# Where the tiles lie: pool order and two fillers in a hybrid attention layer

## The chip, the cores and the metric

The kernel runs on one core of a Trainium2 chip. A time is the device time of one execution in microseconds (us), and the figure compared is the median over runs. TensorE is the matrix engine: a matmul streams its moving operand, up to 512 columns, through a stationary operand ("the weights") that a separate instruction has loaded before. The weights of the next matmul are loaded while the present one streams.

## The reference

One decoder layer over 2048 tokens with 1024 channels, with 16 learned meta tokens ahead of them, all in float32:

```python
xn = rms_norm(h, norm_gain[l])
proj = xn @ w_in[l]
sb_q, sb_k, sb_v, sw_q, sw_k, sw_v, sb_z, sw_z, g_sb, g_sw = jnp.split(proj, offsets, axis=-1)
o_sb = stick_breaking_attention(sb_q, sb_k, sb_v, valid)       # 8 heads of 64, all earlier keys
q, k = rope(sw_q, pos), rope(sw_k, pos)
o_sw = sliding_window_sink_attention(q, k, sw_v, sinks, valid) # 16 query heads, 2 key heads, 128 keys
y_sb = (o_sb * jax.nn.silu(sb_z)) @ w_branch_sb[l]
y_sw = (o_sw * jax.nn.silu(sw_z)) @ w_branch_swa[l]
merged = jax.nn.sigmoid(g_sb) * y_sb + jax.nn.sigmoid(g_sw) * y_sw
h = h + merged @ w_out[l]
return rms_norm(h, final_norm_gain)
```

(The heads' reshapes are left out.) The stick-breaking attention weighs each key by sigmoid(z) times the product of one minus sigmoid(z) over all nearer keys.

## The kernel before, in words

**Precision.** Every large operand is split into a high and a low part (`xh` and `xl`, `wh` and `wl`, and so on), and a product takes three matmuls: low and high of the moving operand with `wh`, and high with `wl` (L400 to L402 in `gemm`). A product of 1024 channels is 8 blocks of three, 24 matmuls of 512 columns.

**Stages.** Tokens come in four groups of 512, in two halves of two groups.
- The opening normalizes the first groups and makes the first keys, queries and values. For a part of it the moving operands are `uh` and `ul`, the rows not yet scaled, in the pool `start`.
- Each half then has a window stage (pool `swa0` or `swa1`): the projections run as the main stream, and `weave` inserts the sliding-window attention between their blocks. Its matmuls are the scores (L695, moving `kk`, weights `q`), transposes of the scores `sc` (L724, moving `ident`) and the values (L741, moving `ph`, `pl`, `ch`, `cl`, weights `vv` for two and difference tiles `xs` for the other two).
- Then a stick stage (pool `sb0` or `sb1`): the gates' projections are the main stream, and the stick-breaking attention is woven in. Its matmuls are the scores (L838, moving `kt`, weights `q1` and `q2`), transposes of `row` (L860), and the values (L886, moving `wth` and `wtl`, weights `vc`).
- The finish, for both halves, projects the two branches (L222 to L224, moving `ringl` for the window branch and `ringr` for the other, weights `wh` and `wl`), merges them into `ringl`, and multiplies by the output weights (L279 to L281, weights `ringl`, moving `ringr`).

**Order.** TensorE's order is written out by hand over the whole program; so is VectorE's until early in the first window stage, and ScalarE's and SP's in the opening. The rest is ordered by a scheduler. SP issues all of the data transfers from one queue.

**Where tiles lie.** A pool hands out places in the order in which its tiles are first asked for, and pools are stacked: `const`, then one of `start`, `swa0`, `sb0`, `swa1`, `sb1` and the finish's `cl` on the left side; `w`, `x`, `tmp` and the finish's `wb` on the right. So what stands at the end of `const` shifts all of the left pools. The right side's `xh`, `xl`, `wh` and `wl` lie at 480 modulo 512 bytes, and `ringr` at 160. `const` ends at 320, and from there the sizes of the tiles set the rest; `row` and `sc` are not whole multiples of 512 bytes long, so each of their buffers lies elsewhere.

Of the kernel before, what the change touches and what calls it, by code (L numbers as in the profile page):

```python
# [7 lines left out]
F32 = mybir.dt.float32  # L8
F32R = mybir.dt.float32r
# [7 lines left out]
P = 128  # L17
# [3 lines left out]
NM = 16  # L21
GT = 512
# [5 lines left out]
QB = 4  # L28
# [11 lines left out]
def f32(ap):  # L40
    return ap.bitcast(F32)
# [3 lines left out]
def tile_kernel(ctx, tc, x, xt, meta, metat, gain, w_in, w_sb, w_sw, w_out, sinks, fgain,  # L45
# [8 lines left out]
    def DMA(dst, src):  # L54
        nc.sync.dma_start(*(t.bitcast(F32) if t.dtype == F32R else t for t in (dst, src)))

    ctx.enter_context(tc.manual_schedule(engines={mybir.EngineType.PE}))
    cp = ctx.enter_context(tc.tile_pool(name="const", bufs=1, side="left"))
# [19 lines left out]
    vn = cp.tile([P, 4], F32, name="vn")  # L78
    vf = cp.tile([P, 16], F32, name="vf")
    mx = cp.tile([P, KT, 48], F32R, name="mx")  # L80
    for t in (vm, mx):
        V.memset(f32(t), 0.0)

# [509 lines left out]
    def window(half, groups, sp):  # L593
# [3 lines left out]
        sn = sp.tile([P, 2 * GT], F32, name="sn")  # L597
        DMA(ct, cost[:, groups[0] * GT:(groups[0] + 2) * GT])
        DMA(sn, sint[:, groups[0] * GT:(groups[0] + 2) * GT])
        if half == 0:  # L600
            cm = sp.tile([P, NM], F32, name="cm")
            sm = sp.tile([P, NM], F32, name="sm")
            DMA(cm, cost[:, SEQ:])
            DMA(sm, sint[:, SEQ:])
            G.memset(f32(kk[:, :, 8 * P:]), 0.0)
            G.memset(f32(vv[:, 8]), 0.0)
        else:
            DMA(kk[:, :, 8 * P:], ksv)
            DMA(vv[:, 8].rearrange("p a d -> p (a d)"), vsv)
# [167 lines left out]
    def stick(groups, bp, sums_of={}):  # L777
        kt, vc = {}, {}
        rows_of = {}
        for g in groups:  # L780
            w = wm[g % 2]
            G.memset(f32(w), 1.0)
            G.affine_select(out=w, in_=f32(w), pattern=[[-1, 4], [0, P]], compare_op=ALU.is_equal, fill=0.0,
                            base=-64 - 4 * g, channel_multiplier=1)
        av_todo = []

        def load_kv(h, g):

            p, a = divmod(h, 2)
            r = slice(64 * a, 64 * a + 64)  # L790
            if h not in kt:
                kt[h] = bp.tile([P, (4 - groups[0]) * GT + NM], F32R, tag="k", name="kt", bufs=2)
            for c in range(g, 4):
                if (h, c) in vc:
                    continue
                c0 = (c - groups[0]) * GT
                cs = slice(c0, c0 + GT + (NM if c == 3 else 0))
                DMA(kt[h][0:64, cs], kd[p][c][0][r])
                DMA(kt[h][64:128, cs], kd[p][c][1][r])
                v = vc[h, c] = bp.tile([P, 4, P], F32R, tag="v", name="vc", bufs=5)  # L800
                DMA(v, vd[p][c][a])
# [13 lines left out]
        def row(h, g, n, j):  # L815

            if n == j == 0:
                load_kv(h, g)
                state[h, g] = {"q": load_q(h, g), "last": {}}
                n1 = len(state) - 1  # L820
                for g1, ssq in list(sums_of.items())[n1 // 8:n1 // 8 + 1]:
                    i, f = divmod(n1 % 8, 2)
                    t = bp.tile([P, GT], F32, tag="q2", name="xq", bufs=2)
                    DMA(t, x[g1 * GT + i * P:g1 * GT + (i + 1) * P, f * GT:(f + 1) * GT])
                    A.activation(t, t, AF.Square, accum_out=ssq[:, f, i:i + 1])
# [70 lines left out]
        n = len(steps)  # L896
        turned = []
        for s in range(n + LT + 3):
# [3 lines left out]
            t = s - LT  # L902
# [181 lines left out]
    for half, groups in enumerate(halves):  # L1084
        with tc.tile_pool(name=f"swa{half}", bufs=1, side="left") as sp:
# [8 lines left out]
            if m:  # L1094
                late_consts()
            sw_k, sw_v, sw_q, attend, ending = window(half, groups, sp)
            q = [[lambda p=p: sw_q(p) for p in (2 * s, 2 * s + 1)] for s in range(4)]
            steps = [(s, g) for s in range(4) for g in groups]
# [26 lines left out]
        with tc.tile_pool(name=f"sb{half}", bufs=1, side="left") as bp:  # L1125
            vsplit[0] = False
            next_sums = {g: sums() for g in halves[1]} if half == 0 else {}
            side = stick(groups, bp, next_sums)
            drain(tiles_by_tile(gts[3:4], groups))
            rest = 25 if half == 0 else 23  # L1130
            cost_sb = 8 * sum(4 * (4 - g) for g in groups) * 1.31 + 16 * 0.75
            ratio = cost_sb / ((rest - 4) * 10.4)
            weave(tiles_by_tile(gts[4:rest], groups), side, ratio)
            drain(side)
            if half == 0:
                t, u = (bp.tile([P, GT], F32, tag="wh", name="sum", bufs=3)[:, :8] for _ in range(2))
                for n, ssq in enumerate(next_sums.values()):
                    V.tensor_tensor(t[:, 4 * n:4 * n + 4], ssq[:, 0], ssq[:, 1], op=ALU.add)
                rs = tp.tile([P, 8], F32, tag="rs8", name="rs", bufs=1)
                rsqrt(rs, t, tp, t=u)  # L1140
                rs0, rs1 = rs[:, :4], rs[:, 4:]
# [72 lines left out]
```

## Time and profile before

| what | value |
|---|---|
| median of 3 runs | 2178.58 us (2178.47 to 2178.74) |
| profiled execution: span, first to last instruction | 2176.8 us |
| what the runs' median has beside the span | 1.8 us |
| TensorE busy | 2148.2 us, 99% |
| VectorE, ScalarE, GpSimd busy | 1355.8, 1007.0, 372.1 us |
| granted TensorE clock, mean | 0.999 |
| opening and first window stage | to about 365 us |
| first gates alone and first stick stage | 365 to 765 us |
| gates and projections, then second window stage | 765 to 1121 us |
| second stick stage | to 1657 us |
| last gates alone | 1657 to 1720 us |
| finish | 1720 us to the end |

A group of instructions is given as line, engine, operation, tiles, shapes and count; then busy time, the mean duration of one in ns, and the idle time ahead of them with what ended it. A row of the timeline gives the start in us, the duration, and the same names. The duration of a matmul includes a modelled end that overlaps the next one, so the time that a matmul costs is the step from its start to the next one's start, not its duration; of two groups of the same shape, though, durations show which one steps faster.

### The profile page before, as it was taken

What the parts mean: (1) busy time and instruction counts of PE and PEld (TensorE: products, weight loads), DVE (VectorE), ACT (ScalarE), POOL (GpSimd) and SP (SyncE); (2) the same over time, 40 slices, a digit from 0 to 9 for tenths busy, and PEclk for the clock granted to TensorE, in tenths of its full rate; (3) what the DMA queues carried; (4) which work ended last, traced back from release to release, by engine and by line L of the source; (5) the groups of instructions that cost most, each with busy time, mean ns of one, the idle gap of its engine ahead of it and who ended that gap; (6) DMA issues with size and microseconds to landing.
All of it is one profiled execution on the core that took longest, in us unless ns stands there. A gap on an engine that the chain in (4) does not pass through costs nothing.

```text
span 2176.8 us, 30232 instructions
## 1 busy us (share of the span) xinstructions
PE 2148.2 (99%) x10614; PEld 1766.2 (81%) x10614; DVE 1355.8 (62%) x2117; ACT 1007.0 (46%) x2328; POOL 372.1 (17%) x486
## 2 busy tenths in 40 slices
PE   8999999999999999999999999999999999999998
PEld 6778888888888888888877888888888888887886
DVE  7687875456555443777746888878774436553453
ACT  6577774344434434777744555555553202221121
POOL 2233342332223200222310000000000232000000
PEclk9999999999999999999999999999999999999999
DMA  9755455765555465444365443333323986468532
GB/s 334 262 179 189 171 188 183 253 200 200 182 187 182 153 203 158 142 165 148 124 193 163 119 122 112 119 100 104 117 85 126 356 276 195 167 218 277 155 97 87
DMA packets 174648, 380.41 MB, mean 175 GB/s; under 512 B 22912, under 2 KB 41088, under 8 KB 174496
## 3 DMA queue, kind: packets, MB, share of 16 engines
q1 hardware_dynamic: 174496, 378.48, 52.2%
q8 instruction: 84, 1.38, 0.3%
q14 instruction: 68, 0.56, 0.1%
HBM read 237.35 MB, written 140.98 MB: 174 GB/s over the span
## 4 chain that ended last, share of the span: by engine, by line
PE 90%; DMA 3%; ACT 3%; DVE 3%; issue 1%; POOL 0%; SPq 0%; ACTq 0%; DVEq 0%; POOLq 0%
PE ps_g L400 15%; PE ps_g L401 14%; PE ps_g L402 14%; PE ps_o L886 6%; PE ps_z L838 6%; PE ps_t L860 5%; PE ps_o L741 2%; PE ps_z L695 2%; PE ps_g L223 1%; PE ps_g L224 1%; PE ps_z L224 1%; PE ps_z L223 1%; PE ps_z L222 1%; PE ps_g L222 1%; PE ps_t L224 1%
## 5 line engine op out<-in xcount | busy, mean ns | idle before, releaser
L400 PE MATMUL ps_g<-xh,wh 128*128 128x512 f32 x1544 | 638.0, 413 | 8.0 <-ACT xh L936 7.6
L402 PE MATMUL ps_g<-xh,wl 128*128 128x512 f32 x1544 | 608.1, 394 | 0.6 <-DVE wl L108 0.6
L401 PE MATMUL ps_g<-xl,wh 128*128 128x512 f32 x1544 | 608.1, 394 | 0.0
L849 DVE TENSOR_TENSOR_SCAN row<-row 128x512 f32<-128x512 f32 (+2 forms) x320 | 371.2, 1162 | 168.8 <-POOL row L847 98.3
L402 PEld LDWEIGHTS ps_g<-xh,wl 128*128 128x128 f32 x1544 | 290.8, 188 | 66.1 <-DVE wl L108 1.1
L400 PEld LDWEIGHTS ps_g<-xh,wh 128*128 128x128 f32 x1544 | 292.2, 189 | 55.2 <-ACT xh L936 7.6
L401 PEld LDWEIGHTS ps_g<-xl,wh 128*128 128x128 f32 x1544 | 292.3, 189 | 43.8 <-DVE xl L937 1.3
L842 ACT ACTIVATE row<-ps_z 128x512 f32<-128x512 f32 (+1 forms) x320 | 171.9, 538 | 251.3 <-PE ps_z L838 208.4
L112 DVE SCALAR_TENSOR_TENSOR wtl<-ps_t,wth 128x512 fp32r<-128x512 f32 (+1 forms) x320 | 190.0, 594 | 46.5 <-ACT wth L111 45.1
L111 ACT ACTIVATE wth<-ps_t 128x512 fp32r<-128x512 f32 (+1 forms) x320 | 170.2, 532 | 91.4 <-PE ps_t L860 89.8
L838 PE MATMUL ps_z<-kt,q 128*128 128x512 f32 (+3 forms) x640 | 185.2, 370 | 0.3 <-ACT row L842 0.3
L860 PE MATMUL ps_t<-ident,row 128*128 128x128 f32 x1088 | 171.7, 273 | 1.2 <-DVE row L849 1.2
L860 PEld LDWEIGHTS ps_t<-ident,row 128*128 128x128 f32 x1088 | 135.9, 140 | 37.3 <-DVE row L849 1.7
L847 POOL TENSOR_SCALAR_AFFINE_SELECT row<-row 128x128 f32<-128x128 f32 x128 | 45.3, 355 | 620.6 <-ACT row L842 548.4
L838 PEld LDWEIGHTS ps_z<-kt,q 128*128 128x128 f32 x640 | 118.8, 188 | 26.3 <-ACT row L842 0.8
L886 PE MATMUL ps_o<-wth,vc 128*128 128x512 f32 (+1 forms) x320 | 125.9, 393 | 1.3 <-DVE tmp L891 1.1
L107 POOL TENSOR_SCALAR wh<-raw 128x1024 fp32r<-128x1024 f32 (+1 forms) x63 | 65.3, 1037 | 330.7 <-PE ps_g L401 213.6
L557 ACT ACTIVATE tmp<-ps_g 128x512 f32<-128x512 f32 x112 | 67.0, 599 | 118.1 <-PE ps_g L402 111.4
L886 PE MATMUL ps_o<-wtl,vc 128*128 128x512 f32 (+1 forms) x320 | 116.9, 365 | 0.0
L703 ACT ACTIVATE sc<-sc,nm 128x129 f32<-128x129 f32 x256 | 100.0, 393 | 35.9 <-DVE nm L701 35.1
L108 POOL TENSOR_TENSOR wl<-raw,wh 128x1024 fp32r<-128x1024 f32 (+1 forms) x43 | 96.3, 2240 | 3.1
L618 POOL TENSOR_TENSOR tmp<-tmp 128x512 f32<-128x512 f32 (+1 forms) x37 | 48.6, 1315 | 202.0 <-DVE tmp L617 84.6
(306 smaller groups left out, 3407.9 us busy)
## 6 DMA issues: line engine op xcount, KB each, us to landing
wh<-h_in_w_in SPq DMA_DIRECT2D x66, 512.0 KB, 3.8
wl<-l_in_w_in SPq DMA_DIRECT2D x66, 512.0 KB, 4.9
raw<-in_w_in SPq DMA_DIRECT2D x50, 512.0 KB, 5.6
h_in_w_in<-wh SPq DMA_DIRECT2D x50, 512.0 KB, 3.7
l_in_w_in<-wl SPq DMA_DIRECT2D x50, 512.0 KB, 2.9
q<-qd SPq DMA_DIRECT2D x128, 128.0 KB, 3.1
vc<-vd SPq DMA_DIRECT2D x48, 256.0 KB, 3.0
kd<-tmp SPq DMA_DIRECT2D x32, 256.0 KB, 4.9
```

Source lines behind the costliest of these rows:

```text
L108: (V if vsplit[0] else G).tensor_tensor(l, src, f32(h), op=ALU.subtract)
L111: A.activation(h, acc, AF.Copy, scale=scale)
L112: V.scalar_tensor_tensor(l, acc, scale, f32(h), op0=ALU.mult, op1=ALU.subtract)
L400: T.matmul(acc, lhsT=wh[:, k, :], rhs=xh[g][:, k, :], start=k == 0, stop=False)
L401: T.matmul(acc, lhsT=wh[:, k, :], rhs=xl[g][:, k, :], start=False, stop=False)
L402: T.matmul(acc, lhsT=wl[:, k, :], rhs=xh[g][:, k, :], start=False, stop=k == KT - 1)
L703: A.activation(sc[:, hh, :], sc[:, hh, :], AF.Exp, bias=nm[:, hh:hh + 1], accum_out=den[:, hh:hh + 1])
L838: T.matmul(z[:, :w], lhsT=lq, rhs=kt[h][:, k0:k0 + w], start=t == 0, stop=t == 1)
L842: A.activation(r[:, :w], z[:, :w], AF.Sigmoid, scale=-1.0)
L849: V.tensor_tensor_scan(r[:, :w], r[:, :w], r[:, :w], last[j] if n else 1.0, op0=ALU.mult, op1=ALU.min)
L860: T.transpose(tr[:, j * P:(j + 1) * P], rows_of[h, g, n - (j > i), j][:, k0:k0 + P], ident)
L886: T.matmul(o[:, :n], lhsT=v, rhs=r, start=first and r is wh, stop=last and r is wl)
```

## The change

Three places are edited. The constant pool gets a tile `mcs` of 40 floats (160 bytes) at its end, which holds the meta tokens' cosines and sines that had two tiles of their own in the first window stage (32 floats; 8 are filler). The window's pool asks for `q`, `ph`, `pl`, `ch`, `cl` and `os` ahead of `sc` and the small tiles, by an allocation of each that nothing uses. The stick stages' pool asks for `vc`, `q1`, `q2`, `wth` and `wtl` ahead of `kt` and `row` in the same way, gives the two buffers of `kt` a tag each, and puts 48 floats (192 bytes, `pad`) between what stands before and the second `kt`.

```diff
@@ in tile_kernel
     mx = cp.tile([P, KT, 48], F32R, name="mx")
+    mcs = cp.tile([P, 40], F32, name="mcs")
@@ in window
         DMA(ct, cost[:, groups[0] * GT:(groups[0] + 2) * GT])
         DMA(sn, sint[:, groups[0] * GT:(groups[0] + 2) * GT])
+        sp.tile([P, 2, GT], F32R, tag="q", name="q", bufs=QB)
+        for t in ("ph", "pl", "ch", "cl"):
+            sp.tile([P, 4, P], F32R, tag=t, name=t, bufs=1)
+        sp.tile([P, 2, GT], F32, tag="os", name="os", bufs=1)
         if half == 0:
-            cm = sp.tile([P, NM], F32, name="cm")
-            sm = sp.tile([P, NM], F32, name="sm")
+            cm, sm = mcs[:, 0:NM], mcs[:, NM:2 * NM]
             DMA(cm, cost[:, SEQ:])
             DMA(sm, sint[:, SEQ:])
@@ in stick
         rows_of = {}
+        bp.tile([P, 4, P], F32R, tag="v", name="vc", bufs=5)
+        for t, name, n in (("q1", "q1", 2), ("q2", "q2", 2), ("wh", "wth", 3), ("wl", "wtl", 3)):
+            bp.tile([P, GT], F32R, tag=t, name=name, bufs=n)
@@ in load_kv
             if h not in kt:
-                kt[h] = bp.tile([P, (4 - groups[0]) * GT + NM], F32R, tag="k", name="kt", bufs=2)
+                if h == 1:
+                    bp.tile([P, 48], F32, name="pad")
+                kt[h] = bp.tile([P, (4 - groups[0]) * GT + NM], F32R, tag=f"k{h % 2}", name="kt", bufs=1)
```

By the addresses of the two built programs, the operands of matmuls then lie as follows (modulo 512 bytes):

| operand | before | after |
|---|---|---|
| `xh`, `xl`, `wh`, `wl` | 480 | 480 |
| `uh`, `ul` (opening) | 320 | 480 |
| `kk`, `vv` (windows) | 320 | 480 |
| `q` (first, second window) | 448, 320 | 480, 480 |
| `ph`, `pl`, `ch`, `cl` (first, second window) | 192, 64 | 480, 480 |
| `xs` as weights of L741 | 320 | 320 |
| `kt` (the two buffers) | 320, 384 | 480, 480 |
| `q1`, `q2`, `vc` | 448 | 480 |
| `wth`, `wtl` | 192 | 480 |
| `row`, eight places 64 apart | 0, 64, 128 ... | 32, 96, 160 ... |
| `ringl` (finish) | 320 | 480 |
| `ringr` (finish) | 160 | 160 |

The order of TensorE, VectorE, ScalarE and GpSimd is the same in both programs. On SP's queue the two small loads move. In the opening before, where `xs_452` is the second half of the fourth 128-row block of `x`, and `raw1` and `tmp` take the transposed `x` of the next group:

```order
L55 DMA xs_451<-in_x 128x512
L55 DMA sel_68<-in_sel 128x128 x2
L55 DMA skb_69<-in_sinks 128x16
L55 DMA xs_452<-in_x 128x512
L55 DMA raw1_499<-in_xt 128x512
L55 DMA raw1_503<-in_xt 128x512
```

and in the changed program:

```order
L55 DMA xs_452<-in_x 128x512
L55 DMA sel_68<-in_sel 128x128 x2
L55 DMA skb_69<-in_sinks 128x16
L55 DMA mcs_76<-in_cost 128x16
L55 DMA xs_453<-in_x 128x512
L55 DMA raw1_500<-in_xt 128x512
```

The cosines' load now stands between the sinks and the second half of the fourth block; the sines' load stands eight transposed loads further on, ahead of the next group's rows of `x`. Later on the same queue before, at the entry to the first window stage (`ct` and `sn` are its cosines and sines, `kd` and `qd` the stored keys and queries):

```order
L55 DMA kd1_2_100<-tmp_758 128x512
L55 DMA ct_842<-in_cost 128x1024
L55 DMA sn_843<-in_sint 128x1024
L55 DMA cm_846<-in_cost 128x16
L55 DMA sm_847<-in_sint 128x16
L55 DMA raw_1081<-in_w_in 128x1024
```

and in the changed program:

```order
L55 DMA kd1_2_101<-tmp_759 128x512
L55 DMA ct_843<-in_cost 128x1024
L55 DMA sn_844<-in_sint 128x1024
L55 DMA raw_1086<-in_w_in 128x1024
L55 DMA kd0_3_98<-tmp_782 128x512
```

The two small loads are gone from here, and the weights of the value projection follow the window's sines.

## Prediction

> **What bounds the kernel now.** I read the page's busy times and its chain that ended last, then TensorE's groups stretch by stretch, then its timeline row by row at the places where operands change.
>
> ```profile
> PE 2148.2 (99%) x10614; PEld 1766.2 (81%) x10614; DVE 1355.8 (62%) x2117; ACT 1007.0 (46%) x2328; POOL 372.1 (17%) x486
> ...
> PE 90%; DMA 3%; ACT 3%; DVE 3%; issue 1%; POOL 0%; SPq 0%; ACTq 0%; DVEq 0%; POOLq 0%
> ```
>
> TensorE sets the end nearly everywhere, so a nanosecond saved per matmul is saved in full as long as its feeders keep up. The step from one matmul's start to the next is therefore the quantity to price. In the timeline, rows that open and close pure runs of 512-column matmuls are:
>
> ```profile
> 1667.03 0.39 PE L400 MATMUL ps_g<-xh,wh 128*128 128x512 f32 x1
> ...
> 1720.07 0.40 PE L222 MATMUL ps_g<-ringl,wh 128*128 128x512 f32 x1
> ...
> 1809.68 0.39 PE L222 MATMUL ps_z<-ringr,wh 128*128 128x512 f32 x1
> ...
> 1854.47 0.40 PE L279 MATMUL ps_t<-ringr,ringl 128*128 128x512 f32 x1
> ...
> 1944.25 0.39 PE L222 MATMUL ps_g<-ringl,wh 128*128 128x512 f32 x1
> ...
> 2035.00 0.39 PE L222 MATMUL ps_z<-ringr,wh 128*128 128x512 f32 x1
> ```
>
> - First to second row: 234 matmuls of the last gates, moving `xh`/`xl` at 480 (always modulo 512 bytes), weights at 480: 53.04 / 234 = **226.7 ns**.
> - Second to third: 8 x 2 x 24 = 384 matmuls, moving `ringl` at 320, weights at 480: 89.61 / 384 = **233.4 ns**.
> - Third to fourth: 192 matmuls, moving `ringr` at 160, weights at 480: 44.79 / 192 = 233.3 ns.
> - Fourth to fifth: 384 matmuls, moving `ringr` at 160, weights `ringl` at 320: 89.78 / 384 = 233.8 ns.
> - Fifth to sixth: 384 of `ringl` with `wh`/`wl` again: 90.75 us, in which TensorE waited 0.6 us:
>
> ```profile
> PE ps_g L222 <- ACT ringl L198: 0.4, 1, 0.4
> ...
> PE ps_g L223 <- DVE ringl L199: 0.2, 1, 0.2
> ```
>
> That leaves 90.15 / 384 = 234.8 ns. So with moving operand and weights at one place a matmul costs 226.7 ns, and some 7 ns more in three mixtures of different places. The Trainium skill, page "TensorE: Matmul & The Clock Gate", section "Step-by-step: what each phase is for", says the opposite of such a dependence: loading the next weights takes no SBUF bandwidth from the running matmul, because the two come through independent read ports. By that rule the change is worth nothing on TensorE; the 226.7 against 233.4 ns here disagree with it, unless something else slows the finish (a rival below).
>
> **The change part by part.** TensorE, VectorE, ScalarE and GpSimd keep their instructions and their order. What changes is where tiles lie, and two small loads on SP's queue.
>
> *The finish.* `ringl` moves from 320 to 480, with `wh`/`wl` staying at 480. Its 768 matmuls as moving operand take the step of the gates: 89.61 - 384 x 0.2267 = 2.57 us, and 90.15 - 87.05 = 3.10 us, together **-5.6 us**. The other 384 projections keep their 160 against 480. The 768 output matmuls (L279 to L281) go from 160 against 320 to 160 against 480, which is the pair of the third to fourth rows: 233.3 instead of 233.8, at most -0.4 us; I take 0. The feeders hold: the two waits above were 0.6 us in 450, and their work stays as it was.
>
> *The opening.* `uh`/`ul` move from 320 to 480 for 72 matmuls.
>
> ```profile
> 22.33 0.39 PE L401 MATMUL ps_z<-xl,wh 128*128 128x512 f32 x1
> ...
> 27.34 0.39 PE L402 MATMUL ps_z<-xh,wl 128*128 128x512 f32 x1
> ...
> 28.23 0.40 PE L401 MATMUL ps_z<-ul,wh 128*128 128x512 f32 x1
> ...
> 33.38 0.39 PE L402 MATMUL ps_z<-uh,wl 128*128 128x512 f32 x1
> ```
>
> Twenty-two steps took 5.01 us with `xh` and 5.15 us with `uh`: 6.4 ns each, 0.46 us over 72. A later wait on VectorE can swallow some; I take **-0.3 us**, ends -0.5 and 0.
>
> *SP's queue.* The loads of the meta tokens' cosines and sines went into tiles of their own in the window's pool; now they go into a constant tile and stand some 40 us earlier, the first ahead of the second half of the opening's fourth `x` block and the `xt` loads, the second ahead of the next `x` rows; both so pass the rest of the opening's loads and the stores of weights, `kd` and `qd`.
>
> ```profile
> 15.52 0.38 SPq L55 DMA_DIRECT2D xs<-in_x  x1
> ...
> 54.76 0.42 SPq L55 DMA_DIRECT2D cm<-in_cost  x1
> 55.23 0.43 SPq L55 DMA_DIRECT2D sm<-in_sint  x1
> ...
> 23.52 0.20 ACT L117 ACTIVATE rs<-ssq 128x4 f32<-128x4 f32 x1 [0.69 <-DVE ssq L116]
> ...
> 23.87 2.55 ACT L936 ACTIVATE uh<-raw,gn 128x512 fp32r<-128x512 f32 x4
> ```
>
> Each issue costs 0.43 us, so the loads behind are late by up to 0.85 us. What hides it: ScalarE's wait ahead of `uh` was for VectorE and not for a load, and it reached `uh` at 23.87, 8 us after SP passed this place; TensorE uses the result from 28.23 on. If that cover were gone the opening would lose 0.85 us; behind 55 us the queue is as much shorter, and the weights queued next come that much sooner. I take 0, ends +0.85 and -0.85.
>
> *Placeholders.* The tiles allocated ahead of use, the 192 bytes of `pad` and the two tags of `kt` add no instruction; each ring keeps its number of buffers. They change which tiles of the window a stick stage's first loads lie on. Those loads go out in SP's unchanged order and have time:
>
> ```profile
> 1132.54 1.17 SPq L55 DMA_DIRECT2D kt<-kd  x2
> ...
> 1157.30 1.09 PE L838 MATMUL ps_z<-kt,q 128*128 128x512 f32 x4
> ```
>
> 25 us lie between the first issue and the first use, and TensorE had no wait ahead of that row: 0. A release later by more than this would cost what exceeds it.
>
> *Both attentions.* There the gates' and projections' own pair already lies at 480/480, yet its durations are longer than in the pure run:
>
> ```profile
> L401 PE MATMUL ps_g<-xl,wh 128*128 128x512 f32 x74 | 28.8, 390 | 0.0
> ...
> L401 PE MATMUL ps_g<-xl,wh 128*128 128x512 f32 x362 | 143.0, 395 | 0.0
> L402 PE MATMUL ps_g<-xh,wl 128*128 128x512 f32 x362 | 142.5, 394 | 0.0
> ...
> L838 PE MATMUL ps_z<-kt,q 128*128 128x512 f32 x334 | 106.4, 399 | 0.0
> L886 PE MATMUL ps_o<-wtl,vc 128*128 128x512 f32 x170 | 67.0, 394 | 0.0
> ```
>
> The first row is the pure run (1657 to 1712 us), the next two the first stick stage (396 to 765), the last two the second (1173 to 1657). So something besides the pair's own places costs 4 to 5 ns there. The timeline shows it behind four transposes within an all-480 run:
>
> ```profile
> 787.24 0.60 PE L359 MATMUL ps_t<-ident,rs 128*128 128x128 f32 x4
> 787.60 0.48 PE L400 MATMUL ps_g<-xh,wh 128*128 128x512 f32 x1
> 787.91 0.40 PE L401 MATMUL ps_g<-xl,wh 128*128 128x512 f32 x1
> ...
> 788.38 0.39 PE L400 MATMUL ps_g<-xh,wh 128*128 128x512 f32 x1
> ...
> 789.77 0.39 PE L400 MATMUL ps_g<-xh,wh 128*128 128x512 f32 x1
> ...
> 791.81 0.39 PE L400 MATMUL ps_g<-xh,wh 128*128 128x512 f32 x1
> ```
>
> From 787.91 to 789.77 eight steps take 1.86 us, 232.5 ns each; the nine after that 2.04 us, 226.7 each. A disturbed stream of one place needs about eight matmuls, and 46 ns, to settle. In the stick stages transposes come at each of 352 steps (320 blocks and 32 turns of the meta tokens), and their groups count some 2820 matmuls of 512 columns: 8 from one disturbance to the next. So they pay the settling now and will pay it after. Only matmuls past the eighth gain: counted along the timeline some 190, times 5 ns: **-0.9 us**. In the windows the four value matmuls run together:
>
> ```profile
> L741 PE MATMUL ps_o<-cl,xs 128*128 128x512 f32 x30 | 12.0, 399 | 0.0
> L741 PE MATMUL ps_o<-pl,vv 128*128 128x512 f32 x30 | 11.9, 398 | 0.2 <-DVE pl L112 0.2
> ...
> L695 PE MATMUL ps_z<-kk,q 128*128 128x256 f32 x256 | 35.5, 281 | 0.0
> ...
> L695 PE MATMUL ps_z<-kk,q 128*128 128x256 f32 x256 | 35.7, 282 | 0.6 <-DVE sc L699 0.6
> ```
>
> `ph` to `cl` move to 480 and `vv` to 480, but the difference tiles `xs` stay at 320, so half of 256 steps match: 128 x 7 ns = **-0.9 us**. `kk` and `q` already shared a place in the second window (last row, 282 ns) and did not in the first (281): matching them is worth +1 ns x 256 = **+0.3 us**. Bounds for both attentions: at the low end every wide matmul (2820 in the stick stages at 5 ns, 1770 in the windows at 3 ns) loses its excess, -19 us; at the high end all of the stick stages' fall to the first two steps above, (788.38 - 787.91) / 2 = 235 ns, 8.3 over the floor instead of 5, +9.9 us. I take the sum of the three, -1.5 us, because the settling row is the nearest to what these stages do.
>
> Sum: -5.6 - 0.3 + 0 - 1.5 = -7.4 us. The profiled execution has a span of 2176.8 us, 1.8 below the runs' median of 2178.58, which holds what lies outside the span; against the median that is **2171.2 us**.
>
> **The rivals.**
> - *The attentions settle at once.* If the settling comes from the neighbours' places and not from the transposes, most of the 19 us goes too. At three quarters of it: 2178.6 - 5.9 - 14 = 2158.7. For: before the change every neighbour of the 480 stream lies elsewhere. Against: the 787 us rows, where all lies at 480. Chance 0.13.
> - *Place does not matter.* The finish may be slow because its banks rotate through g, z and t or because its tiles are freshly written, and not for their places; then nothing changes: 2178.6. This is the time that the rule of the Trainium skill named above gives. Against: `xh` into ps_z stepped at 5.01 / 22 = 228 ns in the opening, settling included. Chance 0.09.
> - *Half is given back.* The finish gains, but the new places make the stick stages' steps 1 ns dearer: 2178.6 - 5.9 + 2.8 = 2175.5. Chance 0.10.
> - *Slower.* A same-place stream is dearest just behind a disturbance (235 ns), and the woven pieces there are often three matmuls long before the next narrow one. At the high end above: -5.9 + 9.9 = +4.0, **2182.6**. It decides the sign from 5.9 us / 2820 = 2.1 ns per stick matmul on. Chance 0.05.
>
> **How the numbers follow.** The forecast has the remaining 0.63, with its own range of 2168.5 to 2174 (attentions -4 to +1). To reach 8 in 10 the range takes in the half given back and part of the first rival: 2163.5 to 2176.5. A change below 0.2%, 4.4 us, can't be told from none here, so faster means under 2174.2: the forecast and the first rival, 0.76, and a little of the third, 0.77. Within: 0.18. Slower: 0.05.
>
> **What would show it.** In the changed kernel the finish's L222 to L224 with `ringl` should read 390 ns, and its first 384 matmuls take 87.1 us instead of 89.6; L279 to L281 should stay near 395; L401 in the stick stages should stay at 394 or 395; L695 of the first window should rise to 282; TensorE should have no new wait in the first 60 us. The forecast is wrong if the finish's rows don't fall, or if the stick stages' move by more than 1 ns either way.

## The result and the profile after

The changed kernel takes **2171.65 us** (median, 2170.32 to 2173.56) against 2178.16 us (2176.91 to 2178.8) for the kernel before in the same measurement: 6.5 us less, ratio 0.997 with a 95% interval of 0.9962 to 0.9979. A second measurement of the same kernel, described below, gave 2172.12 against 2179.21, 7.1 us less. In four of the measurements below one execution took 3 to 9 ms; it stands in the medians, which move by less than 0.6 us without it, and not in the ratios. The profiled execution has a span of 2170.3 us; before it was 2176.8.

All line numbers are up by one in the finish and by four to nine in the attentions. The rows of TensorE's timeline that open the finish's runs (columns: start in us, duration, engine, line, operation):

```profile
1716.25 0.39 PE L223 MATMUL ps_g<-ringl,wh 128*128 128x512 f32 x1
...
1803.29 0.39 PE L223 MATMUL ps_z<-ringr,wh 128*128 128x512 f32 x1
...
1848.09 0.39 PE L280 MATMUL ps_t<-ringr,ringl 128*128 128x512 f32 x1
...
1937.69 0.39 PE L223 MATMUL ps_g<-ringl,wh 128*128 128x512 f32 x1
...
2028.47 0.39 PE L223 MATMUL ps_z<-ringr,wh 128*128 128x512 f32 x1
```

The first half's 384 `ringl` matmuls now take 1803.29 - 1716.25 = 87.04 us, 226.7 ns each, where they took 89.61. The second half's, the fourth to the fifth row, take 90.78; before 90.75. So one half gained all that was there and the other nothing. TensorE's waits in the finish tell where to look (line waited at, releaser: us in total, times, longest):

```profile
PE ps_g L223 <- ACT ringl L199: 0.6, 1, 0.6
...
PE ps_g L224 <- DVE ringl L200: 0.4, 2, 0.2
```

And the timeline of the changed kernel around them (in brackets the idle time ahead and its releaser):

```profile
1957.88 0.39 PE L225 MATMUL ps_g<-ringl,wl 128*128 128x512 f32 x1
1958.24 0.50 PE L223 MATMUL ps_g<-ringl,wh 128*128 128x512 f32 x1
1958.97 0.50 PE L224 MATMUL ps_g<-ringl,wh 128*128 128x512 f32 x1 [0.22 <-DVE ringl L200]
1959.31 0.39 PE L225 MATMUL ps_g<-ringl,wl 128*128 128x512 f32 x1
1960.28 0.50 PE L223 MATMUL ps_g<-ringl,wh 128*128 128x512 f32 x1 [0.57 <-ACT ringl L199]
1961.01 0.50 PE L224 MATMUL ps_g<-ringl,wh 128*128 128x512 f32 x1 [0.23 <-DVE ringl L200]
1961.35 0.52 PE L225 MATMUL ps_g<-ringl,wl 128*128 128x512 f32 x1
1961.66 0.63 PE L223 MATMUL ps_z<-ringl,wh 128*128 128x512 f32 x1
...
1964.65 0.51 PE L224 MATMUL ps_z<-ringl,wh 128*128 128x512 f32 x1
1965.00 0.40 PE L225 MATMUL ps_z<-ringl,wl 128*128 128x512 f32 x1
```

Two losses stand there. From 1957.88 to 1961.35 six steps take 3.47 us instead of 6 x 0.227 = 1.36: the waits cost 2.1 us, about twice the idle time that their records show (0.22 + 0.57 + 0.23). Before, the same place cost 1.2 us. Then, from 1961.66 to 1964.65, seven steps take 427 ns each; with the two partly slow ones around them that is 1.6 us more. The clock was not granted in full, as the windows of the two kernels around their waits show (stretch, length, busy time and count of TensorE, weight loads, VectorE, ScalarE, GpSimd, then granted clock, DMA share, GB/s). The changed kernel:

```profile
1955.00:1968.00 13.00, 11.98 (x43) 8.68 (x42) 6.55 (x11) 3.72 (x6) 0.00 (x0) 0.87 0.91 305
```

The kernel before, whose waits came at 1966.50 and 1967.23:

```profile
1965.00:1980.00 15.00, 14.39 (x61) 11.06 (x60) 6.18 (x10) 3.10 (x5) 0.00 (x0) 1.00 0.95 325
```

So the second half is 384 x 0.2267 + 2.1 + 1.6 = 90.8 us after, and 384 x 0.2333 + 1.2 = 90.8 before.

What comes late is the second group of gated tiles. Their `ringl` places come free with the last output product of the first half, and their operands are loaded by SP's queue into a ring of six `a` tiles, behind the last output rows. In the changed kernel:

```profile
1936.83 0.34 SPq L55 DMA_DIRECT2D out<-res  x1
1937.26 0.38 SPq L55 DMA_DIRECT2D a<-ow  x1
1937.73 0.73 SPq L55 DMA_DIRECT2D a<-zw  x1
```

The loads begin as the first half ends (1937.69), with the DMA engines 91% busy from 1955 to 1968. By this reading a matmul stream that got 6.6 ns a step faster reaches the second group sooner, and the loads do not come sooner; the experiments test it.

The attentions, by the same groups as before. First stick stage:

```profile
L403 PE MATMUL ps_g<-xh,wl 128*128 128x512 f32 x364 | 143.2, 394 | 0.0
L402 PE MATMUL ps_g<-xl,wh 128*128 128x512 f32 x364 | 142.9, 393 | 0.0
```

L402 was L401 and read 395; L403 was L402 and read 394. First window stage:

```profile
L699 PE MATMUL ps_z<-kk,q 128*128 128x256 f32 x256 | 35.7, 282 | 0.0
...
L745 PE MATMUL ps_o<-cl,xs 128*128 128x512 f32 x31 | 12.3, 397 | 0.0
L745 PE MATMUL ps_o<-pl,vv 128*128 128x512 f32 x31 | 12.2, 395 | 0.2 <-DVE pl L113 0.2
```

The three read 281, 399 and 398 before.

Since TensorE's order is the same in both programs, the time from the first matmul of a stage to that of the next compares like with like. "Again" is the second profile of the changed kernel. Differences to the kernel before in us:

| stage | predicted | after | again |
|---|---|---|---|
| ahead of the first matmul | 0 | -1.1 | -0.9 |
| opening | -0.3 | -0.31 | +1.05 |
| both window stages | -0.6 | -0.80 | -0.89 |
| both stick stages | -0.9 | -1.45 | -1.50 |
| gates alone | 0 | -0.11 | +0.47 |
| `ringl` run, first half | -2.57 | -2.57 | -2.57 |
| output product, first half | 0 | -0.19 | +0.53 |
| `ringl` run, second half | -3.10 | +0.04 | -2.04 |
| the rest of the finish | 0 | +0.02 | +0.02 |

Two profiles of one kernel differ by 0.6 to 1.4 us in the opening, the gates alone and the first output product and by 2.1 in the second `ringl` run, so a small term is read only where both agree.

### The profile page after: what moved, and what is told of

The parts are those of the page before. It is cut to its first block, busy times and chain, and to the rows that moved or that the text cites. A ratio compares the mean times of both kernels' runs of the same rounds, so it can differ in the third digit from the quotient of the medians.

```text
span 2170.3 us, 30229 instructions
## 1 busy us (share of the span) xinstructions
PE 2142.2 (99%) x10614; PEld 1765.9 (81%) x10614; DVE 1357.5 (63%) x2117; ACT 1008.5 (46%) x2328; POOL 372.2 (17%) x486
## 4 chain that ended last, share of the span: by engine, by line
PE 88%; DVE 3%; ACT 3%; DMA 3%; issue 2%; POOL 0%; SPq 0%; DVEq 0%; ACTq 0%; POOLq 0%
PE ps_g L401 15%; PE ps_g L403 14%; PE ps_g L402 14%; PE ps_o L895 6%; PE ps_z L847 6%; PE ps_t L869 5%; PE ps_z L699 2%; PE ps_o L745 2%; PE ps_z L223 1%; PE ps_z L224 1%; PE ps_g L224 1%; PE ps_z L225 1%; PE ps_g L225 1%; PE ps_g L223 1%; PE ps_t L225 1%
## 5 line engine op out<-in xcount | busy, mean ns | idle before, releaser
L401 PE MATMUL ps_g<-xh,wh 128*128 128x512 f32 x1544 | 637.9, 413 | 6.9 <-ACT xh L945 6.4
L403 PE MATMUL ps_g<-xh,wl 128*128 128x512 f32 x1544 | 606.4, 393 | 0.6 <-DVE wl L109 0.6
L402 PE MATMUL ps_g<-xl,wh 128*128 128x512 f32 x1544 | 606.4, 393 | 0.0
L403 PEld LDWEIGHTS ps_g<-xh,wl 128*128 128x128 f32 x1544 | 290.5, 188 | 66.3 <-DVE wl L109 1.1
L401 PEld LDWEIGHTS ps_g<-xh,wh 128*128 128x128 f32 x1544 | 291.8, 189 | 54.3 <-ACT xh L945 6.4
L402 PEld LDWEIGHTS ps_g<-xl,wh 128*128 128x128 f32 x1544 | 292.4, 189 | 43.0 <-DVE xl L946 1.3
```

Source lines behind the costliest of these rows:

```text
L401: T.matmul(acc, lhsT=wh[:, k, :], rhs=xh[g][:, k, :], start=k == 0, stop=False)
L402: T.matmul(acc, lhsT=wh[:, k, :], rhs=xl[g][:, k, :], start=False, stop=False)
L403: T.matmul(acc, lhsT=wl[:, k, :], rhs=xh[g][:, k, :], start=False, stop=k == KT - 1)
```

## The experiments

The theory: the place of an operand pair sets the step; the second half's gain was turned into waits for `ringl`, with a clock drop behind them. Each median stands beside that of the kernel before on the same chip.

**`ringl` alone.** The kernel before with

```diff
+        lp.tile([P, 40], F32, name="fill")     # lp: the finish's pool
```

> The kernel before with one edit: 40 floats of filler in the finish's pool, which put ringl at 480 instead of 320; opening and attentions as before. Theory (place decides, and the second half's gain is lost again at a wait for ringl with a clock drop behind it): the first half's 384 ringl matmuls take 87.0 us instead of 89.6, the second half's stay at 90.8 as in the changed kernel, every earlier stage stays within 0.1 us, in all -2.6 us against before (2175.6). Rival, place does not matter and the finish gained from something in the earlier stages: 2178.2, first half 89.6. Rival, the second half's loss belongs to what the attentions' edit did to the transfers: both halves 87.0, -5.7 us, 2172.5.

2174.64 us against 2179.34, ratio 0.9981 (0.9973 to 0.999). The first half's run took 87.04 us and no stage from the windows to the last gates moved by more than 0.15: place decides, without the attentions' part. The second half's run took 88.64, not the expected 90.8: -2.1 us. Its waits were one pair,

```profile
PE ps_g L223 <- ACT ringl L199: 0.6, 1, 0.6
...
PE ps_g L224 <- DVE ringl L200: 0.2, 1, 0.2
```

which cost 1.5 us, and behind them the clock was granted in full:

```profile
1955.00:1968.00 13.00, 12.20 (x52) 9.34 (x51) 7.97 (x13) 3.72 (x6) 0.00 (x0) 1.00 0.93 331
```

So beside the one profile of the kernel before the waits give back 0.4 us, and they come without slow steps too.

**`ringl` back.** The changed kernel with

```diff
+        lp.tile([P, 88], F32, name="fill")     # lp: the finish's pool; ringl at 320 again
```

> The changed kernel with 88 floats of filler in the finish's pool, which put ringl back to 320; opening and attentions stay changed. Theory: the finish as before (89.6 and 90.8 us for its two runs of 384 ringl matmuls), opening -0.3, windows -0.8, stick stages -1.45, together -2.5 us against before plus what of the start's 1.2 us is not chance: between 2174.5 and 2175.7. Rival, the earlier stages' differences are chance from execution to execution: 2178.2. Rival, the finish gains without ringl's place: 2172.8 with 87.0 us in the first half.

2176.01 us against 2179.34, ratio 0.9984 (0.9975 to 0.9994): opening and attentions are worth 3.3 us, somewhat more than the expected 2.5, within the interval. By stage, windows -0.68, stick stages -1.46, as in the changed kernel to 0.12; the first `ringl` run back at 89.61, the second at 91.32. The second was expected at 90.8: with the old step its waits (0.6 and 0.2 us) cost 1.7 us, where they had cost 1.2. So the cost of these waits scatters between executions, whatever the step.

**The changed kernel again.** No edit.

> The changed kernel once more, for a second profile and times beside the others. Theory (the waits for ringl at the start of the second half's second group are always there, but the drop of the clock behind them in the first profile, some 2.2 of the 3.7 us lost there, was that execution's own): the second half's 384 ringl matmuls take 88.6 us, with 1.5 us in waits and no steps of 0.43 us. Rival, the drop belongs to the kernel: 90.8 again with steps of 0.43 us. In both the time lies about 2.0 us below the kernel with ringl put back plus or minus the drop: 2171 to 2172.5.

2172.12 us against 2179.21, ratio 0.9966 (0.9954 to 0.9978). The second half's run took 88.71 us, with the same pair of waits (0.6 and 0.2 us) and no slow steps:

```profile
1955.00:1968.00 13.00, 12.20 (x52) 9.25 (x51) 8.01 (x13) 3.72 (x6) 0.00 (x0) 1.00 0.90 306
```

So the drop does not come with every execution of the kernel. Among the seven profiles with `ringl` in step with the weights and waits at this place it came in two. Both had three waits within 3 us; of the other five two had three or more as well and no drop. What else decides it stays open. Without the drop, the waits lengthened the second `ringl` run by 1.6 to 2.4 us in these profiles, and by 0.7 to 1.7 us in the four in which `ringl` is out of step with the weights (the kernel before, `ringl` back, and two of the places below).

**Two tiles early.** In the changed kernel, two of the eight gated tiles of the last group are loaded and multiplied ahead of the first half's last output rows, into the ring `gt`:

```diff
+                    if half == t0 // 2 - 1 == 0 and g == groups[1]:
+                        for k in range(2):
+                            early[k] = small("gt", 3)
+                            m, z = small("a", AB), small("a", AB)
+                            DMA(m, ow[k][halves[1][1]])
+                            DMA(z, zw[k][halves[1][1]])
+                            V.tensor_tensor(early[k], m, z, op=ALU.mult)
...
+                    for k, t in early.items():
+                        h, l = osw2[k, g2] = ringl(), ringl()
+                        A.copy(h, t)
+                        V.tensor_tensor(l, t, f32(h), op=ALU.subtract)
```

> The changed kernel, in which two of the eight gated tiles of the second half's second group are loaded and multiplied ahead of the first half's last pair of output rows, so that the ring of a has two fewer loads behind them. Theory (the second half's gain was lost to waits for ringl and to the clock that dropped behind them): no wait of TensorE for ringl between 1945 and 1980 us, no matmul steps of 0.43 us there, the second half's 384 ringl matmuls take 87.1 us instead of 90.8, -3.7 us against the changed kernel (about 2168). Rival, the clock drops there by itself (by load, not by the wait): waits gone but still 3.7 us of long steps, 2171. Rival, the waits move to the next ringl tiles since the loads of tiles three to eight come no earlier: some 90 us, 2170 to 2171.

2169.98 us against 2179.34, ratio 0.9958 (0.9943 to 0.9974): 9.4 us less than the kernel before, where the changed kernel had 6.5 and 7.1. The expected further 3.7 us came from the profile with the drop; the medians show 2.3 to 2.9. TensorE has no wait for `ringl` left, and the second half's run takes 87.06 us:

```profile
1938.80 0.39 PE L223 MATMUL ps_g<-ringl,wh 128*128 128x512 f32 x1
...
2025.86 0.39 PE L223 MATMUL ps_z<-ringr,wh 128*128 128x512 f32 x1
```

With the waits the slow steps are gone too, in the same busy transfers:

```profile
1955.00:1968.00 13.00, 13.00 (x59) 10.78 (x58) 6.29 (x10) 2.94 (x5) 0.00 (x0) 1.00 0.97 328
```

The late `ringl` is shown as the cause of the waits: with two loads issued earlier they are gone, and the run is at its floor. That the clock drop needs the waits is likely and not shown: it is missing in the three profiles without waits, and also in five of the seven with them.

**`ringr` in step too.** The changed kernel, with a filler in the right pool before `ringr` is first asked for (160 becomes 480):

```diff
+            if half == 0:
+                cp.tile([P, 48], F32, name="fill")
```

> The changed kernel with 48 floats of filler in the right pool ahead of ringr, which put ringr at 480 instead of 160: the other branch's L223 to L225 (192 matmuls a half) and the output product L280 to L282 (384 a half) then have both operands at 480. Theory (differing places cost 6.7 ns a step): the other branch's runs take 43.5 us each instead of 44.8, the output products 87.1 instead of 89.6 to 89.8, together 1152 x 6.7 ns = -7.7 us, less what is lost to feeders that come late: 2164 to 2167. Rival, what matters is only that the moving operand lies where the weights of the projections lie, not that the pair matches: the output products stay at 89.6, -2.6 us, 2169. Rival, all of it is turned into waits for operands: 2171.

2165.56 us against 2179.34, ratio 0.9939 (0.9926 to 0.9953). The other branch's runs took 43.52 us each (before 44.79), the last output product 86.81 (before 89.37); the first half's took 87.79 with five slow steps in it, and the second half's `ringl` run 89.18, of which 2.1 us are three waits. Outside the slow steps all 1152 matmuls gained the 6.7 ns, so what counts for the output product is the place of its own weights, `ringl`, and not that of `wh`. The groups of the first output blocks and of the other branch:

```profile
L280 PE MATMUL ps_t<-ringr,ringl 128*128 128x512 f32 x96 | 37.3, 389 | 0.0
...
L223 PE MATMUL ps_z<-ringr,wh 128*128 128x512 f32 x48 | 18.7, 389 | 0.0
```

**Both.** `ringr` in step and two tiles early, the two diffs above together.

> Both edits together: ringr at 480, and two of the last group's gated tiles loaded and multiplied early. In the run with ringr at 480 alone the first half's output product lost 0.7 us and the second half's ringl matmuls 2.1 us to waits; in the run with the early tiles alone the second half's ringl matmuls had none. Theory: place and feeders add up: ringl runs 87.05 us each, ringr runs 43.5, output products 87.0 to 87.8, that is 2.1 us less than with ringr at 480 alone (about 2163.5), and 6.4 less than with the early tiles alone. Rival, the early tiles come too late now that TensorE arrives 5 us earlier there: waits come back and it takes 2165 to 2166.

2162.24 us against 2179.21, ratio 0.9919 (0.9906 to 0.9933), a little below the expected sum. No wait in the finish; 87.04, 43.52, 87.04, 87.04, 43.52 and 86.81 us are all at the floor of 226.7 ns.

**The transposes' moving operand in step.** The changed kernel with `const` in another order (`vn`, `vf`, `mcs` ahead of `ident` and `sel`), so that `ident`, `vm` and `wm` lie at 480:

> The changed kernel with the constants' order changed, so that ident (moving operand of all the transposes) and the small operands vm and wm lie at 480 as well; nothing else moves. Theory of the prediction, the transposes disturb the stream of 512 columns whatever their place: the 512-column steps of the first stick stage keep an excess of 4.2 us over 226.7 ns each and those of the second 6.2, time as the changed kernel. Rival, the disturbance comes from a neighbour whose operands lie elsewhere: the stick stages' excess falls by a half or more, -5 us or better, the stages to 366 and 480.5 us.

2170.98 us against 2179.21, ratio 0.9961 (0.9947 to 0.9975). The stick stages took 368.16 and 482.79 us instead of 368.33 and 483.50: a gain of 0.9 us, and the excess of their 512-column steps over 226.7 ns stayed, 4.3 and 5.8 us (4.2 and 6.2 in the changed kernel; every 512-column matmul counts here, whatever follows it). The rival of a disturbing narrow neighbour would have taken half of it.

**Both operands of the transposes in step.** On top of that, in the first stick stage, `row` buffers of 576 floats that start at 224, which is 480 modulo 256:

```diff
+                if h == 0 and groups[0]:
+                    bp.tile([P, 48], F32, name="pad")     # ahead of the first row
...
-            r = bp.tile([P, RW], F32, tag="row", name="row", bufs=12)
+            r = bp.tile([P, 576 if groups[0] else RW], F32, tag="row", name="row", bufs=12)
```

> The kernel with ident at 480, in which in the first stick stage alone each buffer of row is lengthened from 528 to 576 floats and starts at 224 modulo 256 bytes, so that there the transposes too have both operands (moving ident, weights row) at the same place modulo 256. Theory A, the settling behind transposes comes from their own two places: the first stick stage's 512-column steps lose most of their 4.3 us of excess and its narrow steps some of their 14.5, 368.2 becomes 363 to 366 us. Theory B, as the prediction had it, a transpose disturbs the stream whatever its places (its width of 128 columns or the pause at it does): the stage stays within 0.3 us of 368.2. All other stages are as with ident at 480 in both.

2170.55 us against 2178.34, ratio 0.9963 (0.9948 to 0.9978). The stage took 367.89 us, 0.3 less than with `ident` alone; its 512-column steps kept 4.0 us of excess, and its main stream reads

```profile
L402 PE MATMUL ps_g<-xl,wh 128*128 128x512 f32 x365 | 143.2, 392 | 0.0
L403 PE MATMUL ps_g<-xh,wl 128*128 128x512 f32 x364 | 143.1, 393 | 0.0
```

against 393 and 394 with the transposes out of step. In this stage both operands of every matmul, narrow or wide, now lie at equal places modulo 256, and the disturbance stays. Theory B holds: narrow matmuls disturb the stream of 512 columns whatever their places.

**Other places of `ringl`.** The changed kernel with 64, 96 and 8 floats of filler in the finish's pool, for `ringl` at 224, 352 and 0.

> The changed kernel with ringl at 224 instead of 480, 256 bytes off the weights' place; ringr stays at 160. Theory, the place counts modulo 512 bytes: the ringl matmuls of the first half step at 233.3 ns (89.6 us for 384). Rival, it counts modulo 256 or 64 bytes or less: 226.7 ns, 87.05 us. The output products (moving ringr at 160, weights ringl at 224) differ by 64 bytes: 233.3 ns if 64 matter, 226.7 if only modulo 64 counts.

> The changed kernel with ringl at 352, 128 bytes off the weights' 480; ringr stays at 160, 192 bytes off ringl. With ringl 256 bytes off, the first half's ringl matmuls stayed at 226.7 ns, while the output products, whose operands then lay 64 bytes apart, stayed at 233.3. Theory, the place counts modulo 256 bytes: the first half's 384 ringl matmuls take 89.6 us again. Rival, it counts modulo 128: 87.05 us. The output products stay at 89.4 to 89.6 in both.

> The changed kernel with ringl at 0, that is 32 bytes above the weights' place modulo 512, and ringr's 160 then 160 above ringl. With ringr 64 above ringl modulo 256 the output products stepped at 228.9 ns, with all other unequal places at 233.3. Theory, a moving operand a little above the weights modulo 256 pays part of the price: the first half's ringl matmuls step at 227 to 231 ns (87.2 to 88.7 us for 384), the output products (160 above) at 233.3. Rival, only +64 is cheap: 233.3 for both, 89.6 us.

One execution of each: 2172.65, 2173.04 and 2176.92 us, beside medians of the kernel before of 2179.21, 2178.34 and 2178.86. The group of `ringl` into `ps_t` (no waits in it) and that of the output products into `ps_g`, `ringl` at 224:

```profile
L282 PE MATMUL ps_g<-ringr,ringl 128*128 128x512 f32 x80 | 31.6, 395 | 0.0
...
L225 PE MATMUL ps_t<-ringl,wh 128*128 128x512 f32 x80 | 31.1, 389 | 0.0
```

at 352:

```profile
L225 PE MATMUL ps_t<-ringl,wh 128*128 128x512 f32 x80 | 31.6, 395 | 0.0
...
L282 PE MATMUL ps_g<-ringr,ringl 128*128 128x512 f32 x80 | 31.2, 390 | 0.0
```

at 0:

```profile
L282 PE MATMUL ps_g<-ringr,ringl 128*128 128x512 f32 x80 | 31.7, 396 | 0.0
...
L225 PE MATMUL ps_t<-ringl,wh 128*128 128x512 f32 x80 | 31.6, 395 | 0.0
```

With the runs' lengths over 384 matmuls this gives one table over all kernels:

| moving minus weights, modulo 256 bytes | seen in | ns a step |
|---|---|---|
| 0 | `ringl` at 480 or 224 with `wh`/`wl`; `ringr` at 480 | 226.7 |
| 32 | `ringl` at 0 with `wh`/`wl` | 233.3 |
| 64 | `ringr` at 160 with `ringl` at 352 | 228.9 |
| 96 | `ringl` at 320 with `wh`/`wl` | 233.4 |
| 128 | `ringl` at 352 with `wh`/`wl` | 233.3 |
| 160 | `ringr` at 160 with `ringl` at 0 | 234.3 |
| 192 | `ringr` at 160 with `wh`/`wl`, or with `ringl` at 224 | 233.3 |

So in these long runs it is the difference of the two places modulo 256 bytes that counts, and 64 is nearly as good as 0. Three expectations were wrong: that places count modulo 512 (224 would then have paid in full), that the output products stay at 89.4 us or more with `ringl` at 352 (they took 87.90, the 228.9 of the table), and that a small positive difference is cheap (32 pays in full).

**All together.** Both finish edits, `ident` at 480 and the longer `row`.

> All that helped together: ringr at 480, two gated tiles early, ident at 480, and row at 224 modulo 256 in the first stick stage. The finish should take 435.0 us as in the run with ringr and the early tiles, the second stick stage 482.8 instead of 483.5, the first 367.9 instead of 368.3, the first window stage some 0.3 less: 1.4 us below that run's 2162.2, about 2160.8. Rival, the last three differences are chance: 2162.2.

**2159.89 us** against 2178.86, ratio 0.9914 (0.99 to 0.9929), 19 us below the kernel before and 12 below the changed one. Its finish:

```profile
1715.39 0.39 PE L223 MATMUL ps_g<-ringl,wh 128*128 128x512 f32 x1
...
1802.43 0.39 PE L223 MATMUL ps_z<-ringr,wh 128*128 128x512 f32 x1
...
1845.95 0.39 PE L287 MATMUL ps_t<-ringr,ringl 128*128 128x512 f32 x1
...
1932.99 0.39 PE L223 MATMUL ps_g<-ringl,wh 128*128 128x512 f32 x1
...
2020.03 0.39 PE L223 MATMUL ps_z<-ringr,wh 128*128 128x512 f32 x1
```

## Why the prediction was right, and where not

The time was forecast within 0.5 us, and part of that is luck. The forecast difference was -7.4 us, the measured ones -6.5 and -7.1, and the terms were off in opposite directions: the second half's `ringl` run gave 1 us less than forecast where the clock held, and the attentions 0.75 more. Two sums are slightly off: 2.57 and 3.10 make 5.7, not 5.6, and 2820 steps at 3.3 ns (8.3 instead of 5) make 9.3, not 9.9. One reading is wrong: at 787 us not "all lies at 480", since the four transposes there move `ident`, which lay at 128; the two runs that moved `ident` and `row` answer it.

- **The finish, first half, -2.57: exact.** `ringl` into `ps_t` reads 389 ns, and the run alone, undone and moved to other places behaves by its place. The rival that place does not matter falls: 226.7 against 233.3 ns for the same instructions. These steps do not fit the Trainium skill's sentence (page "TensorE: Matmul & The Clock Gate", section "Step-by-step: what each phase is for") that loading the next weights takes no bandwidth from the running matmul; that the weight load is what slows the matmul, no run here isolates.
- **The finish, second half, -3.10: wrong, +0.04 in the profile and -2.0 to -2.1 in two others.** Two steps failed. First the base: the prediction took 0.6 us of recorded waits off and put the remaining 3.10 us down to place. The waits really cost 1.2, for each also stretches the steps beside it, and place was worth 384 x 6.6 ns = 2.56. Second, "the feeders hold ... their work stays as it was": their work stayed, but the waits took 1.6 to 2.4 us with `ringl` in step, against 0.7 to 1.7 out of step. That TensorE's earlier arrival makes the difference is the reading that fits; the two ranges touch. The clock drop of 1.6 us in the first profile came on top.
- **Output products and the other branch, 0:** right in the first profile, -0.19 and 0.01 us; in the second the first half's output product took 0.53 more, in five slow steps ahead of `ringr` matmuls. Both terms' pairs still differed in place, and `ringr` at 480 with two tiles early showed the 7.7 us (2 x 1.27 + 2 x 2.56) that the change had left.
- **Opening, -0.3: not to be told in the time.** From the first matmul to the first of the windows it took 103.2 to 105.4 us in the twelve profiles with the changed opening, and 103.8 and 104.2 us in the two with the old one. In the steps the gain is there: the excess over 226.7 ns of the opening's 512-column matmuls, summed over consecutive starts (steps under 262 ns), is 0.80 and 0.82 us with the old opening and 0.31 to 0.46 in the twelve.
- **SP's loads and the placeholders, 0:** no new wait in the first 60 us of either profile of the changed kernel. The earlier start (-1.1 us; TensorE's first wait, for `xh`, was 6.4 instead of 7.6 us) is no gain of the change: with the old opening and `ringl` alone that wait was 6.8, with the changed one it was up to 7.1.
- **Attentions, -1.5: measured -2.25.** Sorting the steps between 512-column matmuls by their position since the last narrower one gives the excess over 226.7 ns in us (steps under 262 ns, as above):

| position | stick stages, before | after | windows, before | after |
|---|---|---|---|---|
| 1 to 3 | 4.58 | 4.90 | 2.04 | 2.10 |
| 4 to 8 | 3.77 | 2.69 | 1.77 | 1.74 |
| past 8 | 1.11 | 0.27 | 1.31 | 0.51 |

Past the eighth the stick stages gained 0.84 us, where the prediction had 0.9, but from 311 steps at 2.7 ns and not 190 at 5: the product is right by luck. What it missed is the fourth to the eighth step in the stick stages, 1.1 us. The first three pay 0.3 more, a trace of what the slower rival lived on. The windows' terms were mis-sized too, with a sum near the forecast. The prediction's 0.9 was for the 128 value matmuls with `vv`, at 7 ns each; they gained 0.40 us, 3.1 ns each. The other 128, with `xs`, gained 0.20, and the projections past the eighth 0.45, where the prediction had nothing. `kk` with `q` in the first window costs 0.2 us more, as forecast (0.3).

By kind, the gain of the stick stages does not follow the matmuls' own places. Summed from start to start, the scores, whose places came into step, gained 0.26 us; the values, `wth` at 192 with `vc` at 448 and so already equal modulo 256, gained 0.51; and the gates and projections, at 480 in both kernels, 0.79. The second window agrees: `ph` and `pl` at 64 with `vv` at 320, equal modulo 256 as well, stepped at 231.9 ns before and at 227.8 with all at 480 (61 steps under 262 ns). So here something else counts, perhaps the place of the stream ahead; no run tests it.

Of the rivals of the attentions, settling at once falls in size: 12.2 us of excess remain of 14.6, and moving `ident` and `row` did not take it away. The steps did not get dearer in sum, as half given back and slower would have had it.

- **L401 to stay at 394 or 395:** its group (now L402) reads 393 in both stick stages, and in the first it had read 395. By the prediction's own sign, rows that move by more than 1 ns, its account of the stick stages was wrong: the step that failed is that steps before the ninth would "pay the settling now and will pay it after" in full. L695 of the first window (now L699) rose to 282 as said.

## What to carry to other kernels

When a matmul stream runs a constant few nanoseconds above its floor, compare the byte addresses of its moving operand and its weights modulo 256, pair by pair, and move a pool by a small filler; for these float32 matmuls of 512 columns it is worth 6.6 ns in 233 where they follow each other in long runs, and little where narrow ones break the stream every few steps. Then ask of every speed-up what TensorE now reaches sooner: here the waits for one ring's loads, which start with the end of the previous half, cost 1.6 to 2.4 us until two of the loads were issued earlier. And read a short recorded wait at one and a half times to twice its length (0.6 us cost 1.2, 0.8 cost 1.5, 1.0 cost 2.1).

## What the hardware showed that was not expected

- In the finish's long runs the step depends on the difference of the two operands' places modulo 256 bytes, measured at seven differences: 226.7 ns at 0, 228.9 at 64, 233.3 to 234.3 at the others. Why 64 is cheap and 32 is not stays open. In the short pieces of the attentions the rule alone does not tell the step: pairs that agreed modulo 256 in both kernels still gained, 231.9 to 227.8 ns in the second window.
- After narrow matmuls a stream whose operands agree (in the windows but for the value matmuls with `xs`) steps some 6 ns above its floor for three steps, 3 ns up to the eighth and 1 ns after (the table above divided by its 826, 819 and 311 steps, and 352, 658 and 503). In the first stick stage it did so with all of the narrow ones' places in agreement too.
- Three waits that together idle TensorE for 1.0 us within 3.5 us were followed, in two of the four profiles that had them at this place, by some 3.5 us of steps of 427 ns, with a granted clock of 0.87 over the 13 us around them. The Trainium skill, page "TensorE: Matmul & The Clock Gate", section "Part 1: The HAM clock gate (the "warmup" mystery)", gives 426.7 ns for 512 columns at the half clock and windows of about 3.4 us, which these rows agree with. By the same section of the Trainium skill the half clock comes after at least one idle window; these rows show none, for the longest recorded wait was below 0.6 us.
